# Key/query products in column strips, and the eight decay and gate columns computed from unsplit x, in a DeltaNet/HGRN2 layer on one core

## The chip, the cores and the metric

One NeuronCore of a Trainium2 chip runs the whole program in one launch. The metric is the device time of one execution in microseconds. The kernel before takes 2658.93 us, the median of three runs (2653.82 to 2660.26). Differences under about 0.3% (8 us) can't be told from no change with a few runs.

## The reference

One layer over 2048 tokens of width 1024. Its first part, where all of the change lies, is this (shapes: `GDN_HEADS` = 4, `HEAD_DIM` = 128, the DeltaNet works in chunks of 64 in the reference and of 128 in the kernel):

```python
hn = rms_norm(h, pre_mix_norm[i])
proj = jnp.einsum('btd,dc->btc', hn, w_in[i])     # 32 blocks of 128 columns, and 4 + 4 more
a_gdn = proj[..., OFF_GDN_A:OFF_GDN_B]            # 4 columns: decays
b_gdn = proj[..., OFF_GDN_B:OFF_HG_F]             # 4 columns: gates
...
beta = sigmoid(b_gdn)
g_dec = -exp(gdn_a_log[i]) * softplus(a_gdn + gdn_dt_bias[i])
gc = cumsum(g_dec)                                # inside each chunk
decay = exp(where(causal, gc[..., :, None] - gc[..., None, :], -inf))
lmat = einsum('bhncd,bhnsd->bhncs', k * beta, k) * decay   # only its strictly lower part is used
qk = einsum('bhncd,bhnsd->bhncs', q, k) * decay            # lower triangular
```

The DeltaNet heads, four HGRN2 heads (chunked too), an output projection, a squared-ReLU MLP of width 4096 and a gated embedding follow; the change does not touch what they compute.

## The kernel before

**Stages.** The tokens are worked in four quarters of 512 (`q`). First an embedding product runs while x is loaded and normed (lines L201, L439, L174/L175). Then comes the mixing stage: a list `works` holds, for each quarter, 1 + 8 x 4 = 33 products of the normed x with 128 columns of weights (`mm`, L1167). Output projection and MLP follow (L1050, L1200).

**A split product.** Weights and x are kept as a high and a low part (`split`: one ScalarE copy, L174, and one VectorE difference, L175), so a work is 8 x 3 = 24 matmuls of 128x512. The first work of each quarter, `ab`, has the eight columns of decays and gates in a block of 128 columns that are otherwise zero; it costs a whole work. In quarter 0 the weights are split and the split pair is stored (`cached`); later quarters reload 1 MB for each work.

**The clock.** Each work is three steps of eight matmuls. After every step `tick()` (after half a step `half()`) lets generators go on that stand in an `agenda` under that step: the recurrences of the eight heads (`gdn_mixer`, `hgrn_mixer`), loading of the next quarter's x (`load_x`), sums of MLP weights for later (`down_sums`), and `decays`. TensorE's and SyncE's order is the order of this code; ScalarE's, VectorE's and GpSimd's is set by a scheduler. `A_STEPS`, `B_STEPS`, `A_FIRST` and the like are the step offsets of the generators; a head has 24 steps.

**Full products and strips.** A 128x128 float32 matmul uses the whole array. `strip(g, ...)` is a float32 matmul with 32 stationary columns that lands on 32 rows of the result (`tile_position=(0, 32 g)`); the HGRN2 levels (`at_all`) and the DeltaNet solver (`psp`, `pst`, `psx`, `psd`) already use strips, four next to each other. In before, the k k and k q products of a head (`kk`, L688 and L689) are eight full 128x128 matmuls, and the HGRN2 diagonal (`at_h_d`, L884) is one full 128x256. A float32 matmul shows as two records in the trace.

**PSUM.** Eight banks: `pm` 2 (works), `pp` 3 (everything short: `kk`, `at_h_d`, transposes), `at_all` 1, `po` 2 (the output sums `pso` of a DeltaNet and of an HGRN2 head, in turn).

**Decays.** `decays` (L524 to L548) takes the sum of work `ab` as rows of 4 x 512: bias, softplus by Exp and Ln, tanh for the gates, a cumulative sum in four scans (L533), a store `gd` to DRAM from which each head reads its row as `gf` (L636), and four transposes `ps_gb` (L544) for the column form `gcol`.

Of the kernel before, what the change touches and what calls it, by code (L numbers as in the profile page):

```python
# [10 lines left out]
F32 = mybir.dt.float32  # L11
# [53 lines left out]

A_FIRST = (3, 7, 8, 8, 9, 10, 12, 14) + tuple(range(16, 24)) + (24, 26, 29, 32, 34, 36, 37)
# [30 lines left out]
def trunk(ctx, tc, x, xT, pT, vecs, w_in, w_ab, gdn_a_log, gdn_dt_bias, w_out, w_up, w_down,  # L97
# [12 lines left out]
    po = ctx.enter_context(tc.tile_pool(name="po", bufs=2, space=PSUM))  # L110
# [11 lines left out]
    V.memset(at_all, 0.0)  # L122
# [3 lines left out]
    dec = cp.tile([4, 2], F32, name="dec")  # L126
# [15 lines left out]
    nexpa = cp.tile([4, 1], F32, name="nexpa")  # L142

    def vectors():

        ps = bank("ps_rows", pp)
        PE.transpose(ps[:, :N_ROWS], rows, ident[:N_ROWS, :N_ROWS])
        V.tensor_copy(cols, ps[:, :N_ROWS])
        V.tensor_scalar(ple_w, cols[:, R_PLE : R_PLE + KD], 0.5, None, ALU.mult)
        V.tensor_tensor(lb, lg, lg, ALU.subtract)  # L150
        S.activation(lb, lb, AF.Exp)
        V.reciprocal(lb1, lb)
        V.tensor_tensor(lb, lb, lb1, ALU.mult)
        V.tensor_tensor(lb, lb, lb, ALU.subtract)
# [3 lines left out]
        S.activation(nexpa, dec[:, 0:1], AF.Exp)  # L158
        V.tensor_scalar(nexpa, nexpa, -1.0, None, ALU.mult)
# [227 lines left out]

    with ExitStack() as ectx:
        es = ectx.enter_context(tc.tile_pool(name="es", bufs=1))
        with tc.manual_schedule(engines={mybir.EngineType.SP, mybir.EngineType.Activation, mybir.EngineType.DVE}):  # L390
# [9 lines left out]
            nc.sync.dma_start(dec[:, 0:1], gdn_a_log.rearrange("o h -> h o"))  # L400
            nc.sync.dma_start(dec[:, 1:2], gdn_dt_bias.rearrange("o h -> h o"))
# [51 lines left out]
            while len(xts[0]) < KD:  # L453
                put_x()
            for f in stores:
                f()


    with mixers as mctx:
# [57 lines left out]
        gb = mt("gb", "gb", 1, (36, QT))  # L517
        V.memset(gb, 0.0)

        def decays(ps, q):  # L520

            sp = m2.tile([4, QT], F32, tag="tmp", name=f"sp_{q}")
            se = m2.tile([4, QT], F32, tag="th", name=f"se_{q}")
            S.activation(sp, ps[0:4, :], AF.Identity, bias=dec[:, 1:2])  # L524
            S.activation(gb[32:36, :], ps[32:36, :], AF.Tanh, scale=0.5)
            V.tensor_scalar(gb[32:36, :], gb[32:36, :], 0.5, 0.5, ALU.mult, ALU.add)
            V.scalar_tensor_tensor(se, sp, -1.0, sp, ALU.mult, ALU.max)
            S.activation(se, se, AF.Exp, scale=-1.0)
            S.activation(se, se, AF.Ln, bias=1.0)
            V.scalar_tensor_tensor(sp, sp, 0.0, se, ALU.max, ALU.add)  # L530
            V.tensor_scalar(sp, sp, nexpa, None, ALU.mult)
            for c in range(NC):
                V.tensor_tensor_scan(gb[0:4, blk(c)], one[0:4, :], sp[:, blk(c)], 0.0, ALU.mult, ALU.add)  # L533
            gd = dr.tile([4, QT], F32, name=f"gd{q}")
            decay[q] = [gd, None]
            yield
            nc.sync.dma_start(gd, gb[0:4, :])
            yield
            back = mt(f"gbb_{q}", "gbb", 1, (36, QT // 2))
            V.tensor_copy(back.rearrange("p (n b i) -> p n b i", b=NB, i=SB), odd_back(gb))  # L540
            yield
            ps = bank(f"ps_gb_{q}", ph)
            for c in range(NC):
                PE.transpose(ps[:, c * 36 : (c + 1) * 36], back[:, blk(c // 2)] if c % 2 else gb[:, blk(c)],  # L544
                             ident[:36, :36])
            gcol = sm.tile([P, NC, 36], F32, tag="gcol", name=f"gcol_{q}", bufs=2)
            V.tensor_copy(gcol.rearrange("p c n -> p (c n)"), ps[:, : NC * 36])
            V.tensor_scalar(gcol[:, :, 4:8], gcol[:, :, 0:4], -1.0, None, ALU.mult)  # L548
            decay[q][1] = gcol
# [81 lines left out]
        def gdn_mixer(q, h, live):  # L631
# [4 lines left out]
            nc.sync.dma_start(flat(gf), decay[q][0][h : h + 1, :].broadcast_to([P, QT]))  # L636
# [3 lines left out]
            beta = gcol[:, :, 32 + h : 33 + h].rearrange("p c o -> p (c o)")  # L640
# [43 lines left out]
            for c in range(0, NC, 2):  # L684
                ps = bank(f"kk_{n}_{c}", pp).rearrange("p (a b i) -> p a b i", a=2, b=2)
                for a in range(2):
                    sl = blk(c + a)
                    PE.matmul(ps[:, a, 0, :], kT[:, sl], kT[:, sl], start=True, stop=True)  # L688
                    PE.matmul(ps[:, a, 1, :], kT[:, sl], qT[:, sl], start=True, stop=True)  # L689
# [119 lines left out]
            pso = bank(f"pso_{n}", po)  # L809
# [40 lines left out]
        def hgrn_mixer(q, h, live):  # L850
# [26 lines left out]
            for lev, s in enumerate(LEVELS):  # L877
# [4 lines left out]
                if lev == 1:  # L882
                    ps0 = bank(f"at_{n}_d", ph)[:, : QT // 2]
                    PE.matmul(ps0, one, own, start=True, stop=True)  # L884
                    near = [slice(j * SB // 2, (j + 1) * SB // 2) for j in range(NB)]
                    ps1 = at_all.rearrange("p (c n) -> p c n", c=NC)
# [62 lines left out]
            pso = bank(f"pso_{n}", po)  # L949
# [64 lines left out]
        STEPS = SPT = 3  # L1014
        for q in range(NQ):
            works.append((f"ab{q}", "ab", w_ab, q, None, None, None, None))
# [61 lines left out]
        def load_x(q):  # L1078
# [11 lines left out]
            def ready(k):  # L1090
                t = ra.tile([P, 2, QT], F32R, tag="ring", name=f"xt{q}_{k}")
                split(t, V, raws.pop(k))
                xts[q].append(t)
# [18 lines left out]
            for k in range(2, KD):  # L1112
                ready(k)
                if k % 2:
                    yield

# [19 lines left out]
        per_q = SPT * (1 + 8 * 4)  # L1136
# [3 lines left out]
        for q in range(1, NQ):  # L1140
            at(per_q * (q - 1) + 30, x_scale(q), range(0, 22, 2))
            at(per_q * q, load_x(q), range(-9, 0))
            call(per_q * q, boundary)
        for q in range(2):
            at(0, norm_steps(accs[q], 1.0 / D, EPS, f"e{q}", partial(ple_r.__setitem__, q)),
               [4 * q + i for i in (0, 2, 4, 5, 6)])
        with tc.manual_schedule(engines={mybir.EngineType.SP}):
# [5 lines left out]
            for j, (name, key, src, q, h, then, g, b) in enumerate(works):  # L1153
# [9 lines left out]
                for s in range(SPT):  # L1163
# [4 lines left out]
                    if s == SPT - 1 and h is None:  # L1168
                        at(clock[0], decays(ps, q), (0, 2, 3, 5) if q else (0, 2, 4, 7))
                    tick()  # L1170
                    if s == SPT - 1 and h is not None:
                        then(ps, q, h, g, b)
# [10 lines left out]
    pp = ctx.enter_context(tc.tile_pool(name="pq", bufs=4, space=PSUM))  # L1183
    ctx.enter_context(tc.tile_pool(name="pad", bufs=1)).tile([P, 48], F32, name="pad")
# [790 lines left out]
```

## Time and profile before

| what | value |
|---|---|
| median of three runs | 2658.93 us |
| the profiled execution | 2650.4 us, span 2648.3 us |
| granted TensorE clock, mean | 0.998 |
| busy: TensorE, VectorE, ScalarE, GpSimd | 99%, 74%, 55%, 5% |
| records of matmuls | 14729 |
| mean DMA rate | 217 GB/s |

The page's busy time of TensorE is a union of modelled spans, so the end of each matmul overlaps the next one's start; what one matmul costs in a row of them is read from the distance of starts in the timeline. In a merged row of the timeline the first number is the start of its first record and "x16" the number of records.

### The profile page before, as it was taken

Reading aid. Unit: us, or ns where it says so; the run is one execution under the profiler, and the core shown is the slowest. Engines: PE = TensorE matmul, PEld = TensorE weight load, DVE = VectorE, ACT = ScalarE, POOL = GpSimd, SP = SyncE. Lnnn points to the kernel's source line nnn. Section 1 sums busy time; section 2 is a strip of 40 time slices with the busy share of each in tenths; the row PEclk is TensorE's granted clock in tenths of the full one; section 3 lists DMA queues with packets and bytes.
Section 4 is the critical chain, followed back from the end, with each engine's and each line's share of the span. In section 5 each row is a group of like instructions: output and inputs, shape, how many; then the busy total and the mean of one; then the engine's idle time right before and its main releaser. Section 6 shows DMA issues by size and latency. Waiting matters only on the chain.

```text
span 2648.3 us, 42218 instructions
## 1 busy us (share of the span) xinstructions
PE 2615.3 (99%) x14729; PEld 2159.7 (82%) x14729; DVE 1967.0 (74%) x4030; ACT 1467.4 (55%) x2991; POOL 138.1 (5%) x147
## 2 busy tenths in 40 slices
PE   8999999999999999999999999999999999999999
PEld 6788788888888888887888888888888888888887
DVE  7778777786777777678988778767877765477775
ACT  7676655565456555565666555555554555565431
POOL 0000000000000000110000000001000001101000
PEclk9999999999999999999999999999999999999999
DMA  7878777667667775773765476665644375677663
GB/s 275 273 254 274 249 252 261 226 224 255 218 212 243 226 230 175 212 229 123 235 212 197 171 238 222 215 208 194 207 159 169 138 247 186 199 251 253 202 225 127
DMA packets 267780, 573.75 MB, mean 217 GB/s; under 512 B 55578, under 2 KB 60152, under 8 KB 250416
## 3 DMA queue, kind: packets, MB, share of 16 engines
q1 hardware_dynamic: 265264, 566.86, 64.3%
q0 software_dynamic: 2304, 4.20, 0.9%
q8 instruction: 116, 1.90, 0.3%
q14 instruction: 96, 0.79, 0.1%
HBM read 410.57 MB, written 160.37 MB: 216 GB/s over the span
## 4 chain that ended last, share of the span: by engine, by line
PE 67%; DVE 3%; DMA 3%; issue 2%; ACT 1%; POOL 0%; SPq 0%; DVEq 0%; POOLq 0%; ACTq 0%
PE d L1200 23%; PE u L1200 23%; PE mm L1167 9%; PE mmg L1200 7%; PE mmo L1050 1%; PE mme L201 1%; DMA ud_g<-u_g 0%; DMA mixT<-mixd 0%; DMA yo<-in_xT_dram 0%; DMA xs<-in_x_dram 0%; POOL yo L1286 0%; DVE t L175 0%; DVE acc_o L244 0%; PE psc_g L823 0%; PE psa_g L813 0%
## 5 line engine op out<-in xcount | busy, mean ns | idle before, releaser
L1167 PE MATMUL mm<-xt,w 128*128 128x512 f32 x3072 | 785.4, 401 | 1.0 <-DVE w L175 0.9
L1167 PEld LDWEIGHTS mm<-xt,w 128*128 128x128 f32 x3072 | 552.6, 188 | 105.6 <-DVE w L175 1.7
L1200 PE MATMUL d<-db,da 128*128 128x512 f32 x2688 | 612.9, 389 | 0.0
L1200 PE MATMUL u<-t,wu 128*128 128x512 f32 x2604 | 591.2, 389 | 0.0
L1200 PEld LDWEIGHTS d<-db,da 128*128 128x128 f32 x2688 | 504.7, 188 | 104.6
L1200 PEld LDWEIGHTS u<-t,wu 128*128 128x128 f32 x2604 | 488.9, 188 | 101.3
L228 DVE TENSOR_TENSOR db<-db 128x512 fp32r<-128x512 f32 x224 | 159.8, 713 | 56.0 <-ACT db L227 55.2
L1598 DVE TENSOR_TENSOR u<-u,u 128x512 f32<-128x512 f32 x224 | 150.9, 685 | 53.0 <-PE u L1200 51.1
L1200 PE MATMUL mmg<-h2T,wg 128*128 128x512 f32 (+1 forms) x792 | 174.7, 383 | 0.0
L227 ACT ACTIVATE db<-db 128x512 fp32r<-128x512 f32 x224 | 141.0, 629 | 60.8 <-DMA db<-hid 57.2
L1200 PEld LDWEIGHTS mmg<-h2T,wg 128*128 128x128 f32 x792 | 145.6, 188 | 29.0
L1641 ACT ACTIVATE u<-u 128x512 f32<-128x512 f32 x128 | 80.7, 630 | 153.4 <-DVE u L1598 152.6
L175 DVE TENSOR_TENSOR da<-da 128x512 fp32r<-128x512 f32 x128 | 94.8, 740 | 89.6 <-ACT da L174 87.6
L174 ACT ACTIVATE da<-da 128x512 fp32r<-128x512 f32 x128 | 80.6, 629 | 127.2 <-DMA da<-sumd 105.4
L1200 PE MATMUL mmo<-mixT,w_out 128*128 128x512 f32 x600 | 138.5, 390 | 3.3 <-DVE w_out L175 1.7
L1200 PEld LDWEIGHTS mmo<-mixT,w_out 128*128 128x128 f32 x600 | 112.2, 188 | 28.6 <-DVE w_out L175 3.0
L174 ACT ACTIVATE wu<-a 128x512 fp32r<-128x512 f32 x124 | 75.0, 623 | 58.0 <-DMA a<-in_w_up_dram 55.7
L175 DVE TENSOR_TENSOR wu<-a,wu 128x512 fp32r<-128x512 f32 x124 | 86.3, 697 | 8.5 <-ACT wu L174 7.9
L175 DVE TENSOR_TENSOR da<-dr,da 128x512 fp32r<-128x512 f32 x96 | 68.3, 712 | 26.5 <-ACT da L174 25.4
L1642 ACT ACTIVATE u<-u 128x512 f32<-128x512 f32 x128 | 80.4, 628 | 3.0
L174 ACT ACTIVATE da<-dr 128x512 fp32r<-128x512 f32 x96 | 60.5, 630 | 33.6 <-DMA dr<-in_w_down_dram 26.8
L244 POOL TENSOR_TENSOR acc_y<-acc_y,sq_y 128x512 f32<-128x512 f32 x28 | 38.1, 1362 | 759.2 <-ACT sq_y L243 759.2
(394 smaller groups left out, 3722.7 us busy)
## 6 DMA issues: line engine op xcount, KB each, us to landing
w<-cache_in SPq DMA_DIRECT2D x96, 1024.0 KB
db<-hid SPq DMA_DIRECT2D x224, 256.0 KB
cache_in<-w SPq DMA_DIRECT2D x32, 1024.0 KB
hid<-u SPq DMA_DIRECT2D x128, 256.0 KB
da<-sumd SPq DMA_DIRECT2D x128, 256.0 KB
a<-in_w_up_dram SPq DMA_DIRECT2D x124, 256.0 KB
hid<-ht SPq DMA_DIRECT2D x96, 256.0 KB
dr<-in_w_down_dram SPq DMA_DIRECT2D x96, 256.0 KB
```

The lines of the kernel that those rows point to most:

```text
L174: S.activation(t[:, 0], raw, AF.Copy)
L175: eng.tensor_tensor(t[:, 1], raw, t[:, 0], ALU.subtract)
L201: PE.matmul(ps, a, b, start=i == 0, stop=i == n - 1)
L227: S.activation(t[:, 0], plain(t), AF.Copy)
L228: V.tensor_tensor(t[:, 1], plain(t), t[:, 0], ALU.subtract)
L244: eng.tensor_tensor(acc, acc, sq, ALU.add)
L1050: PE.matmul(ps, w[:, term // 2, k, :], xin[q][k][:, term % 2, :], start=i == 0, stop=i == 3 * KD - 1)
L1167: PE.matmul(ps, *terms[i], start=i == 0, stop=i == nt - 1)
L1200: PE.matmul(ps, a, b, start=start, stop=stop)
L1598: V.tensor_tensor(c[new], c[old], ps, ALU.add)
L1641: S.activation(c[k], c[k], AF.Relu)
L1642: S.activation(c[k], c[k], AF.Square)
```

## The change

1. The works `ab` go: 32 works in a quarter instead of 33 (`per_q` 99 to 96 steps), with their weight split, store and three reloads of 1 MB.
2. `few_columns` takes their place: for each 128 rows of x it runs four strips, one for each 128 tokens, with 32 stationary columns (`w_few`, of which 8 matter) and 128 moving columns of unsplit, float32 x. In quarter 0 these are 8 x 4 strips on the raw x at the end of the embedding; later 10 x 4 (the first two rows of x are taken as two halves each), one step before the quarter begins. The result has the tokens' four blocks on partitions 0, 32, 64 and 96.
3. `decays` works on that 128 x 128 form: one scan instead of four, the gates by Exp of the softplus instead of tanh, two copies on GpSimd and four 128x128 transposes. It is stepped at -0.5, 1 and 3 of the quarter (`FEW_STEPS`) instead of 2, 4, 5 and 7; `gf` is read as four 512-byte rows for each partition.
4. `kk`: eight full matmuls become 32 strips, each only as wide as the causal triangle needs (128, 96, 64, 32 columns), into two fixed banks `of_g` and `of_h`. These replace `po`: the DeltaNet output sum is always in `of_g`, the HGRN2 one in `of_h`. The HGRN2 diagonal becomes four strips of 64 columns into `of_h`.
5. `load_x` of the next quarter is stepped from -11 on instead of -9 (`X_STEPS`); its raw x is held until `few_columns` has read it.

```diff
+FEW_FIRST = (0, 2, 5)
+FEW_STEPS = (0.5, 2, 4)
+X_STEPS = (-11, -10, -9, -7, -6, -5, -3, -2, -1)
...
+    po = mixers.enter_context(tc.tile_pool(name="po", bufs=1, space=PSUM))
+    of_g, of_h = (po.tile([P, QT], F32, name=f"of_{n}") for n in "gh")
...
+    def few_columns(q, terms):
+
+        ps = bank(f"few_{q}", pp)[:, :P]
+        for i, (k, x) in enumerate(terms):
+            for c in range(NC):
+                PE.matmul(ps[c * SB : (c + 1) * SB, :], w_few[:, k * 8 : k * 8 + SB], x[:, blk(c)], start=i == 0,
+                          stop=i == len(terms) - 1, tile_position=(0, c * SB), skip_group_check=True)
+        return ps
...
+            few_first = few_columns(0, [(k, xraw[:, k]) for k in range(KD)])
...
+            sp, se, sums, beta = (mt(f"{n}_{q}", n, 1, (P, P)) for n in ("gsp", "gse", "gsum", "gbeta"))
+            S.activation(sp, ps, AF.Identity, scale=sign, bias=dec[:, 1:2])
             V.scalar_tensor_tensor(se, sp, -1.0, sp, ALU.mult, ALU.max)
             S.activation(se, se, AF.Exp, scale=-1.0)
             S.activation(se, se, AF.Ln, bias=1.0)
             V.scalar_tensor_tensor(sp, sp, 0.0, se, ALU.max, ALU.add)
+            S.activation(beta, sp, AF.Exp, scale=-1.0)
             V.tensor_scalar(sp, sp, nexpa, None, ALU.mult)
-            for c in range(NC):
-                V.tensor_tensor_scan(gb[0:4, blk(c)], one[0:4, :], sp[:, blk(c)], 0.0, ALU.mult, ALU.add)
+            V.tensor_tensor_scan(sums, one, sp, 0.0, ALU.mult, ALU.add)
...
             for c in range(0, NC, 2):
-                ps = bank(f"kk_{n}_{c}", pp).rearrange("p (a b i) -> p a b i", a=2, b=2)
-                for a in range(2):
-                    sl = blk(c + a)
-                    PE.matmul(ps[:, a, 0, :], kT[:, sl], kT[:, sl], start=True, stop=True)
-                    PE.matmul(ps[:, a, 1, :], kT[:, sl], qT[:, sl], start=True, stop=True)
+                ps = (of_h if c else of_g).rearrange("p (a b i) -> p a b i", a=2, b=2)
+                for b, src in enumerate((kT, qT)):
+                    for a in range(2):
+                        for g in range(NB)[:: -1 if a else 1]:
+                            first = slice(g * SB, P)
+                            if a:
+                                first = slice((NB - 1 - g) * SB, P) if b else slice(0, (g + 1) * SB)
+                            strip(g, ps[rows_of(g), a, b, first], kT[:, blk(c + a)][:, rows_of(g)], src[:, blk(c + a)][:, first])
...
-                    ps0 = bank(f"at_{n}_d", ph)[:, : QT // 2]
-                    PE.matmul(ps0, one, own, start=True, stop=True)
+                    ps0 = of_h[:, : QT // 2]
                     near = [slice(j * SB // 2, (j + 1) * SB // 2) for j in range(NB)]
+                    for j in range(NB):
+                        strip(j, ps0[rows_of(j)].rearrange("p (c n) -> p c n", c=NC)[:, :, near[j]], one[:, :SB],
+                              own.rearrange("p (c n) -> p c n", c=NC)[:, :, near[j]])
...
-            works.append((f"ab{q}", "ab", w_ab, q, None, None, None, None))
...
-        per_q = SPT * (1 + 8 * 4)
+        per_q = SPT * 8 * 4
...
-            at(per_q * q, load_x(q), range(-9, 0))
+            at(per_q * q, load_x(q), X_STEPS)
```

On TensorE, at the end of the embedding (`mme`) and the start of quarter 0, before:

```order
L201 MATMUL mme_7_546<-pT_1_363,w_plea_366 128x512 x3
L1167 MATMUL mm_ab_629<-xt_0_460,w_ab_614 128x512 x3
L1167 MATMUL mm_ab_629<-xt_1_477,w_ab_614 128x512 x3
L1167 MATMUL mm_ab_629<-xt_2_494,w_ab_614 128x512 x3
L1167 MATMUL mm_ab_629<-xt_3_511,w_ab_614 128x512 x3
```

and now, at the same place:

```order
L205 MATMUL mme_7_559<-pT_1_376,w_plea_379 128x512 x3
L397 MATMUL few_578<-xraw,w_few 32x128 x32
L1201 MATMUL mm_0_0_677<-xt_0_473,w_0_0_662 128x512 x3
L1201 MATMUL mm_0_0_677<-xt_1_490,w_0_0_662 128x512 x3
L1201 MATMUL mm_0_0_677<-xt_2_507,w_0_0_662 128x512 x3
```

The 24 matmuls on the split x (`xt`) have become 32 strips on the raw x, and the first head's own product follows at once.

On TensorE, before the k k and k q products of the second DeltaNet head of quarter 0, before (the rows ahead are the solver's and the HGRN2 strips of the head before):

```order
L629 MATMUL psx_g_0_1434<-part_582,xt_g_0_1206 32x32 x2
L629 MATMUL at_all<-qk_h_0_983,keys_h_0_3_1392 32x2x16 x8
L688 MATMUL kk_g_1_0_1473<-y_kg_1_1221 128x128
L689 MATMUL kk_g_1_0_1473<-y_qg_1_1297,y_kg_1_1221 128x128
L688 MATMUL kk_g_1_0_1473<-y_kg_1_1221 128x128
L689 MATMUL kk_g_1_0_1473<-y_qg_1_1297,y_kg_1_1221 128x128
```

and now (the first ten rows; 24 strips more follow):

```order
L654 MATMUL psx_g_0_1469<-part_628,xt_g_0_1245 32x32 x2
L654 MATMUL at_all<-qk_h_0_1022,keys_h_0_3_1427 32x2x16 x8
L654 MATMUL of_g<-y_kg_1_1260 32x128
L654 MATMUL of_g<-y_kg_1_1260 32x96
L654 MATMUL of_g<-y_kg_1_1260 32x64
L654 MATMUL of_g<-y_kg_1_1260 32x32
L654 MATMUL of_g<-y_kg_1_1260 32x128
L654 MATMUL of_g<-y_kg_1_1260 32x96
L654 MATMUL of_g<-y_kg_1_1260 32x64
L654 MATMUL of_g<-y_kg_1_1260 32x32
```

The products stand where they stood, right behind other strips, and each row of results has its own width.

On SyncE, where quarter 1's x is loaded, before (`raw_0_3` and `cache_in` are weights of quarter 0, `w_ab` and `w_1_0` reloads for quarter 1, `sys_g` and `ud_g` the solver's):

```order
L711 DMA sys_g_3_3097<-ud_g_3_3054 128x1x1024
L190 DMA cache_in_3109<-w_0_3_2912 128x2048
L255 DMA rsb_x_3121<-rd_x_1865 128x512
L1085 DMA raw_xt_0_3123<-in_xT_dram 128x512
L1085 DMA raw_xt_1_3125<-in_xT_dram 128x512
L620 DMA mixd_1_103<-og_g_1_2763 128x512
L1101 DMA raw_xt_2_3170<-in_xT_dram 128x2x512
L1101 DMA raw_xt_4_3172<-in_xT_dram 128x2x512
```

and now:

```order
L259 DMA rsb_x_3176<-rd_x_2001 128x512
L1115 DMA raw_xt_0_3178<-in_xT_dram 128x512
L1115 DMA raw_xt_1_3180<-in_xT_dram 128x512
L740 DMA sys_g_3_3209<-ud_g_3_3161 128x1x1024
L1131 DMA raw_xt_2_3211<-in_xT_dram 128x2x512
L1131 DMA raw_xt_4_3213<-in_xT_dram 128x2x512
L1115 DMA raw_xt_6_3219<-in_xT_dram 128x512
L194 DMA cache_in_3231<-w_0_3_2997 128x2048
```

The loads stand two steps earlier, now ahead of that weight store and around the solver's load instead of behind both; `raw_xt_4` takes the buffer of the quarter's last raw weights.

More of the change, by code (lines that the diff above doesn't have):

```diff
@@ L808, in gdn_mixer @@
             yield
-            pso = bank(f"pso_{n}", po)
+            pso = of_g
             for c in range(NC):
@@ L1113, in load_x @@
                 ready(k)
-                if k % 2:
+                if k % 2 and k + 1 < KD:
                     yield
+            halves = [(k, xts[q][k].bitcast(F32)[:, i, :]) for k in (0, 1) for i in range(2)]
+            at(clock[0], decays(few_columns(q, halves + [(k, raws[k]) for k in range(2, KD)]), q), FEW_STEPS)
+            yield
         def down_sums(g):
```

75 lines of the change are left out of this document (42 added, 33 removed).

## The prediction

> **What bounds the kernel now.** The page's head and its first part come first, then the busy time by stretch of the run, then who kept TensorE waiting.
>
> ```profile
> span 2648.3 us, 42218 instructions
> PE 2615.3 (99%) x14729; PEld 2159.7 (82%) x14729; DVE 1967.0 (74%) x4030; ACT 1467.4 (55%) x2991; POOL 138.1 (5%) x147
> 47.00:1023.00 976.00, 964.86 (x7278) 798.73 (x7278) 733.62 (x2096) 569.98 (x1480) 57.63 (x72) 1.00 0.73 242
> ```
>
> The last row is the mixing stage, where the whole change lies: 976 us, of which TensorE (first busy column) is free for 11 us. VectorE is busy 75% of it and ScalarE 58%, the granted clock is 1.00. The longest waits of TensorE by what ended them (total, times, longest):
>
> ```profile
> PE kk_g L689 <- ACT y_qg L576: 3.1, 4, 1.2
> PE psc_g L823 <- ACT w_g L820: 2.2, 2, 1.2
> PE kk_g L688 <- DVE xn_g L792: 2.0, 1, 2.0
> PE psp_g L629 <- DMA xn_g<-xd_g: 1.1, 1, 1.1
> ```
>
> So this stage is a full TensorE queue: work taken out of it should show nearly one for one, until the others become late. The sum is therefore one of TensorE time. It is made on the profiled execution (span 2648.3, time 2650.4 us), which lies 8.5 us under the median of 2658.93 and 3.4 us under the fastest of the three; I carry the difference over to the median.
>
> **Prices.** A split matmul of 512 columns:
>
> ```profile
> 2140.99 54.56 PE L1200 MATMUL d<-db,da 128*128 128x512 f32 x240
> ```
>
> is 0.227 us (54.56 less its tail, by 240). Full and strip float32 matmuls stand side by side here:
>
> ```profile
> 618.69 3.12 PE L1167 MATMUL mm<-xt,w 128*128 128x512 f32 x13
> 621.74 0.43 PE L629 MATMUL psp_g<-xn_g,um 128*32 128x64 f32 x16
> 621.99 0.31 PE L629 MATMUL at_all<-qk_h,keys_h 128*32 128x32 f32 x16
> 622.23 0.49 PE L688 MATMUL kk_g<-y_kg 128*128 128x128 f32 x2
> 622.55 0.39 PE L689 MATMUL kk_g<-y_qg,y_kg 128*128 128x128 f32 x2
> ...
> 623.89 0.39 PE L689 MATMUL kk_g<-y_qg,y_kg 128*128 128x128 f32 x2
> 624.04 2.33 PE L1167 MATMUL mm<-xt,w 128*128 128x512 f32 x9
> ```
>
> From 622.55 to 623.89 six full calls (two records each) start: 0.223 us a call, 1.74 ns a column. The 16 records of `psp_g` are eight strips of 64 columns, in 0.25 us: four such strips take 0.125 us, against 0.112 for one full call of that width. Strips in four column groups thus run at the same time, at 1.12 times the cost of one. Going into strips and back costs: 13 works' matmuls from 618.69 end at 621.64, the second `kk` call starts at 622.55, so the first would have stood at 622.33 in a row; of these 0.69 us the strips need 0.25 and about 0.13, and 0.31 is the change of mode. I use 0.33.
>
> **The works that go.** 4 x 24 x 0.227 = 21.8 us. The groups by line put them higher, since busy time holds the tails:
>
> ```profile
> L1167 PE MATMUL mm_ab<-xt,w_ab 128*128 128x512 f32 x96 | 24.6, 397 | 0.2 <-ACT sq_e L243 0.2
> L688 PE MATMUL kk_g<-y_kg 128*128 128x128 f32 x128 | 26.0, 285 | 2.0 <-DVE xn_g L792 2.0
> L689 PE MATMUL kk_g<-y_qg,y_kg 128*128 128x128 f32 x128 | 25.2, 278 | 3.1 <-ACT y_qg L576 3.1
> L884 PE MATMUL at_h_d<-att_h,one 128*128 128x256 f32 x32 | 9.5, 378 | 0.0
> ```
>
> I take 21.8. Their split, store and reloads (1 MB each) also go; neither was on the path, so that counts nothing.
>
> **The eight columns as strips.** 32 strips in quarter 0 and 3 x 40 after it: 152, or 38 sets of four, each 128 columns wide. No row shows strips of 128 columns. From below a set costs one full call, 0.223; from above four calls one after another, 0.89. I take 1.03 calls, near the 64-column row, as its 12% look like a fixed few ns: 38 x 0.23 = 8.7 us. Four entries and exits more, 1.3 us: together +10.0. The sets are one step ahead of the quarter, on x that was scaled four steps before, so they wait for nothing else.
>
> A rule speaks against so full an overlap. The Trainium skill, "TensorE: Matmul & The Clock Gate", Measured speedup vs the span model, has four row tiles 3.07 and three column tiles 2.38 times as fast as one by one, so some 1.26 to 1.3 calls for a set; by it this term would be about 11 us and not 8.7. The trace has 1.12 at 64 columns, which is better than the rule.
>
> **The HGRN2 diagonal.** Its full call of 256 columns is two of 0.223 = 0.446 us, and strips follow it at once, so no change of mode is added:
>
> ```profile
> 607.90 0.59 PE L884 MATMUL at_h_d<-att_h,one 128*128 128x256 f32 x2
> 608.42 0.46 PE L629 MATMUL at_all<-hb_h,qk_h 128*32 128x32 f32 x32
> ```
>
> Four strips of 64 columns cost the 0.125 of `psp_g`. 16 heads x 0.32 = -5.1 us.
>
> **The k k and k q products.** Now 8 x 0.223 = 1.79 us a head. As strips, two blocks give each column group 128 + 32 or 96 + 64 = 160 columns: 0.28 us if the groups run apart, 0.45 if each set of four waits for its widest. This row speaks for apart:
>
> ```profile
> 799.46 0.20 PE L629 MATMUL pst_g<-xt_g,part 128*32 128x32 f32 x3
> 799.48 0.22 PE L629 MATMUL at_all<-qk_h,keys_h 128*32 128x32 f32 x1
> 799.50 0.20 PE L629 MATMUL pst_g<-xt_g,part 128*32 128x32 f32 x2
> ```
>
> `at_all` is behind all `pst` in the program, and yet its first record starts before the last `pst`: a group that has less to do runs ahead. Four pairs: 1.12 to 1.79 us; I take 1.2, near the free end, so 16 x 0.59 = -9.4 us. In nearly all heads other strips stand directly ahead, so only one change of mode is added (+0.3).
>
> **Moved and hidden.** The new transposes are four of 128x128, as in the first row below, 0.36 us up to the next; the old four took 0.37. Even.
>
> ```profile
> 774.23 0.60 PE L597 MATMUL t_ih<-cst,iT_h 128*128 128x128 f32 x4
> 774.59 2.09 PE L1167 MATMUL mm<-xt,w 128*128 128x512 f32 x8
> 796.90 0.25 PE L544 MATMUL ps_gb<-cst,gb 36*128 36x36 f32 x1
> 797.27 0.50 PE L1167 MATMUL mm<-xt,w 128*128 128x512 f32 x1
> ```
>
> The decays' chain is what may now be late. Before, it ran from
>
> ```profile
> 783.86 0.66 ACT L524 ACTIVATE sp<-mm_ab,dec 4x512 f32<-4x512 f32 x1
> 785.16 1.28 ACT L528 ACT_TABLE_LOAD   x1
> 787.70 1.28 ACT L529 ACT_TABLE_LOAD   x1
> 791.33 1.35 DVE L533 TENSOR_TENSOR_SCAN gb<-one,sp 4x128 f32<-4x128 f32 x4
> ```
>
> to 792.68, 8.8 us, with 4 us in hand ahead of `ps_gb` at 796.90. Now operations have 128 columns instead of 512 and there is one scan (0.34), but one table load more (1.28) and the GpSimd copies: some 7 us. The transposes come 3.5 steps behind, at 976 / 396 = 2.46 us a step 8.6 us. Behind them on TensorE waits everything. It fits, narrowly; if the cover is gone, up to 3 us at each of three quarters.
>
> SyncE loads quarter 1's x into the buffer of the last raw weights, whose split is a step later; it stands there for about 2.5 us, with reloads behind it that are needed four steps later. I count nothing.
>
> The fixed banks could make TensorE wait for a reader. The DeltaNet sum was read here, and the products of the next but one head, which will share its bank, start here:
>
> ```profile
> 793.69 0.67 DVE L610 TENSOR_TENSOR og_g<-pso_g,zt_zg 128x512 f32<-128x512 f32 x1
> 810.88 0.39 PE L688 MATMUL kk_g<-y_kg 128*128 128x128 f32 x2
> ```
>
> 16.5 us lie between, three steps fewer now: still 9 us. Nothing.
>
> **Sum.** -21.8 + 10.0 - 5.1 - 9.4 + 0.3 = -26.0 us. The stage gets 2.7% shorter with almost the same work on VectorE and ScalarE, so its 11 us of waits will grow: +2.5, a guess at a fifth of them. Forecast: 23.5 us off, 2627 for a profiled execution and **2635** for the median.
>
> **Rivals.**
> - *Strips of 128 columns overlap only in part, or sets wait for their widest strip.* For it: no row has unequal strips or such wide ones. Against it: the run-ahead row. Strip work is 28 us at full overlap (8.5 + 16 x (1.12 + 0.11)); at 1.3 times that the gain is 8 us less, with the widest-strip rule for `kk` 9 us less: 2644. Chance 0.14. The skill's 2.38 and 3.07 above would give about this.
> - *Strips are held one after another by their issue or by the array: slower.* The place is the 32 strips of each head and the 38 sets. With 28 us at full overlap and 26 us of gain, the change breaks even where strips take 1.9 times as long as assumed; fully one by one (4 times) it costs 84 us more: 2717. Against it: 16 `psp_g` records in 0.25 us. Chance 0.06. The Trainium skill, same page, "Wait — 56ns, not 53.3ns?", has about 62 ns for each MATMUL with hardware decode off; for 1456 records that is 90 us. The trace disagrees: 16 ns a record.
> - *The decays' chain or the loads at the quarter's edge are late.* 3 us for the transposes and 1 to 2 for x at three edges: 12 us, 2647. Chance 0.06.
> - *The gain is taken back by VectorE at 75%* (or the change shifts less than it says): within 8 us of before. It would need waits of 18 us where there are 11 now. Chance 0.04.
>
> **How the numbers follow.** Forecast 0.70 and the rivals as above. About 0.3%, 8 us, is what can be told from no change: faster means under 2651. All of the forecast's 0.70, the first rival's 0.14 and two thirds of the third give 0.88; same 0.06; slower 0.06. The range goes from full overlap without new waits (-27.3, and the 5 us that the lowest run lies under the median, with a little for waits that vanish) at 2624 to the third rival with a margin, 2651; it leaves out the slower case, the last and some of the rest.
>
> **What would show it.** In the changed profile: no `mm_ab`; sets of four `few` strips 0.23 us apart; a head's 64 records of products within 1.1 to 1.3 us, where 1.8 would be the widest-strip case; `at_all` 0.13 us behind the diagonal; TensorE's free time in the stage still under 15 us; and `ps_gb` not waiting for GpSimd by more than 1 us. It is wrong if the stage is not some 20 us shorter, or if a wait on `of_g`, `of_h` or `ps_gb` shows over 3 us.

## The result, and the profile after

The change made the kernel slower: 2773.2 us in the median of four runs, against 2657.0 of the kernel before on the same chip, a ratio of 1.0444 (95% interval 1.0429 to 1.0459). The forecast was 2635. The head of the page of the changed kernel, profiled in a run of 2773.0 us:

```profile
span 2771.3 us, 44339 instructions
...
PE 2666.0 (96%) x15801; PEld 2165.9 (78%) x15801; DVE 1957.5 (71%) x4016; ACT 1467.6 (53%) x2996; POOL 142.4 (5%) x162
```

The busy time by stretch, first of the kernel before, then of the changed one. The first row of each goes from the first to the last matmul `mm` of the mixing stage, the second from there to the end. The first `ab` work before (41.07 to 46.64 us) and the first `few` strips now (43.55 to 45.44) lie ahead of these rows, so of the four `ab` works the first row holds three. The columns are length, then busy time of TensorE, its weight loads, VectorE, ScalarE and GpSimd, then granted clock, DMA share and GB/s.

```profile
47.50:1023.50 976.00, 965.02 (x7279) 798.84 (x7278) 733.62 (x2095) 569.88 (x1481) 57.13 (x68) 1.00 0.73 242
1023.50:2648.30 1624.80, 1614.47 (x7330) 1335.39 (x7328) 1197.80 (x1874) 865.09 (x1453) 77.52 (x64) 1.00 0.60 200
```

```profile
45.40:1120.10 1074.70, 990.53 (x8310) 806.18 (x8307) 724.70 (x2082) 571.62 (x1489) 63.06 (x86) 0.96 0.67 216
1120.10:2771.30 1651.20, 1643.67 (x7336) 1337.98 (x7334) 1199.54 (x1876) 865.91 (x1453) 77.03 (x64) 1.00 0.60 197
```

Two different things show. The mixing stage is 98.7 us longer: TensorE stands free for 84 us in it where it was 11, and the clock is 0.96. The rest, whose work the change does not touch, is 26.4 us longer, at clock 1.00 and with no more free time of TensorE than before (7.5 us, and 10.3 before).

**The strips themselves came out as forecast.** TensorE's timeline of the changed kernel, at the `few` strips of a quarter, at the 64 records of a head's products and at the HGRN2 diagonal (start, length, line, operation):

```profile
298.80 0.87 PE L1201 MATMUL mm<-xt,w 128*128 128x512 f32 x3
299.60 1.08 PE L397 MATMUL few<-xt,w_few 128*32 128x128 f32 x32
300.49 1.49 PE L397 MATMUL few<-raw_xt,w_few 128*32 128x128 f32 x48
301.92 1.19 PE L1201 MATMUL mm<-xt,w 128*128 128x512 f32 x4
...
615.72 0.31 PE L654 MATMUL at_all<-qk_h,keys_h 128*32 128x32 f32 x16
615.84 0.47 PE L654 MATMUL of_g<-y_kg 128*32 128x128 f32 x16
616.12 0.47 PE L654 MATMUL of_g<-y_qg,y_kg 128*32 128x128 f32 x16
616.40 0.47 PE L654 MATMUL of_h<-y_kg 128*32 128x128 f32 x16
616.68 0.47 PE L654 MATMUL of_h<-y_qg,y_kg 128*32 128x96 f32 x16
617.08 0.73 PE L1201 MATMUL mm<-xt,w 128*128 128x512 f32 x2
...
668.20 0.32 PE L654 MATMUL of_h<-att_h,one 128*32 128x64 f32 x8
668.34 0.48 PE L654 MATMUL at_all<-hb_h,qk_h 128*32 128x32 f32 x32
```

The 80 records are 40 strips of two records each, ten sets of four, in 2.32 us: 0.23 us a set. The products take 1.24 us a head (615.84 to 617.08), the diagonal 0.14 us.

**Where the mixing stage waits.** The waits of TensorE that grew most (total, times, longest), and ScalarE's wait for `gf`, before and after:

```profile
PE psc_g L852 <- ACT w_g L849: 44.1, 11, 6.4
PE psa_g L842 <- DVE S_g L854: 12.0, 7, 3.8
PE nrm_g L286 <- DVE hl_g L179: 5.4, 3, 4.4
```

```profile
ACT cd_g L645 <- DMA gf_g<-gd: 4.3, 3, 1.9
```

```profile
ACT cd_g L671 <- DMA gf_g<-gd: 104.4, 16, 10.2
```

VectorE stands for `gf` as well, 64.6 us at `tail_g`.

One of them in the timelines of SyncE's queue, ScalarE and TensorE:

```profile
630.18 0.47 SPq L662 DMA_DIRECT2D gf_g<-gd  x1
```

```profile
634.91 1.28 ACT L671 ACT_TABLE_LOAD   x1
645.75 0.21 ACT L671 ACTIVATE cd_g<-gf_g 128x4 f32<-128x4 f32 x1 [9.55 <-DMA gf_g<-gd]
...
648.26 0.34 ACT L849 ACTIVATE w_g<-psb_g,cc_g 128x128 f32<-128x128 f32 x1
```

```profile
641.76 1.18 PE L1201 MATMUL mm<-xt,w 128*128 128x512 f32 x4
648.66 0.79 PE L852 MATMUL psc_g<-w_g,kt_g 128*128 128x128 f32 x2 [5.71 <-ACT w_g L849]
```

`gf` of the next head is issued at 630.18 and is there at 645.7. ScalarE reaches `cd_g`, which reads it, at 636.2 and stands for 9.55 us. The next instruction of the current head's chain, `w_g`, is queued behind it on ScalarE: the product `psb_g` that it reads was done at 640.2, and it starts at 648.26. `psc_g` behind `w_g` stops TensorE for 5.7 us. So a load of the next head holds up the recurrence of this one.

**The clock adds to such waits.** Of a shorter wait, the row of TensorE and the stretches ahead of it and behind it:

```profile
985.17 0.49 PE L852 MATMUL psc_g<-w_g,kt_g 128*128 128x128 f32 x2 [1.97 <-ACT w_g L849]
```

```profile
980.00:983.00 3.00, 3.00 (x19) 2.45 (x18) 2.32 (x11) 0.41 (x2) 0.00 (x0) 1.00 0.65 203
986.20:989.50 3.30, 3.30 (x13) 3.00 (x12) 2.71 (x8) 1.38 (x5) 0.00 (x0) 0.50 0.89 341
```

After 1.97 us of waiting the granted clock is 0.50 for 3.4 us. Not each such wait has this effect: e1_row (below) has two of 2.0 and 2.1 us, and its clock stays at 1.00 behind both. The changed kernel has 17 such stretches of 3.4 to 10.2 us, each behind one or two waits; past the first 40 us, the kernel before has none up to its last matmul. They make 88.7 us, of which TensorE works 73.0; at half the clock some 36 us of that are lost, an estimate from these two figures. The Trainium skill, "TensorE: Matmul & The Clock Gate", HAM oscillation — how this bites in real kernels, warns of gaps above some 3.4 us; here 2 us were enough.

**The second half** has no new waits to show, only slower matmuls. One long row of it, before and after:

```profile
1849.04 292.11 PE L1200 MATMUL u<-t,wu 128*128 128x512 f32 x1288
```

```profile
1957.92 298.48 PE L1233 MATMUL u<-t,wu 128*128 128x512 f32 x1288
```

The same 1288 matmuls are 226.7 ns apart before and 231.6 ns after.

### The profile page after: what moved, and what is told of

It reads as the page before. It is cut to its first block, busy times and chain, and to the rows that moved or that the text cites. A ratio compares the mean times of both kernels' runs of the same rounds, so it can differ in the third digit from the quotient of the medians.

```text
span 2771.3 us, 44339 instructions
## 1 busy us (share of the span) xinstructions
PE 2666.0 (96%) x15801; PEld 2165.9 (78%) x15801; DVE 1957.5 (71%) x4016; ACT 1467.6 (53%) x2996; POOL 142.4 (5%) x162
## 4 chain that ended last, share of the span: by engine, by line
PE 53%; DVE 2%; issue 2%; DMA 2%; ACT 1%; POOL 0%; SPq 0%; DVEq 0%; POOLq 0%; ACTq 0%
PE u L1233 22%; PE d L1233 21%; PE mmg L1233 6%; PE mmo L1080 1%; PE mme L205 1%; DMA mixT<-mixd 0%; DMA sys_g<-ud_g 0%; DMA b<-h1d 0%; DMA yo<-in_xT_dram 0%; DVE acc_o L248 0%; POOL yo L1319 0%; DVE t L179 0%; DMA rd_g<-m_g 0%; DMA yod<-yo 0%; DVE w_out L179 0%
## 5 line engine op out<-in xcount | busy, mean ns | idle before, releaser
L1201 PE MATMUL mm<-xt,w 128*128 128x512 f32 x3072 | 819.1, 412 | 7.5 <-DVE w L179 2.5
L1201 PEld LDWEIGHTS mm<-xt,w 128*128 128x128 f32 x3072 | 567.9, 194 | 124.8 <-issue 4.4
L1233 PE MATMUL d<-db,da 128*128 128x512 f32 x2688 | 621.5, 392 | 0.1
L1233 PE MATMUL u<-t,wu 128*128 128x512 f32 x2604 | 604.0, 394 | 0.0
L179 DVE TENSOR_TENSOR wu<-a,wu 128x512 fp32r<-128x512 f32 x124 | 85.8, 694 | 10.6 <-ACT wu L178 10.4
```

Source lines behind the costliest of these rows:

```text
L179: eng.tensor_tensor(t[:, 1], raw, t[:, 0], ALU.subtract)
L1201: PE.matmul(ps, *terms[i], start=i == 0, stop=i == nt - 1)
L1233: PE.matmul(ps, a, b, start=start, stop=stop)
```

## The experiments

**1. What makes `gf` late.** The change stores the running sums as 128 rows of 128, so `gf` is read as four rows of 512 bytes per partition, 16,384 bytes apart in DRAM, where it was one row of 2 KB. Run e1_row puts the old form into the changed kernel:

```diff
-            gd = dr.tile([P, P], F32, name=f"gd{q}")
+            gd = dr.tile([4, QT], F32, name=f"gd{q}")
-            nc.sync.dma_start(gd, sums)
+            for c in range(NC):
+                nc.sync.dma_start(gd[:, blk(c)], sums[c * SB : c * SB + 4, :])
-            nc.sync.dma_start(gf, bass.AP(gd.tensor, gd.offset + h * P, [[0, P], [SB * P, NC], [1, P]]))
+            nc.sync.dma_start(flat(gf), decay[q][0][h : h + 1, :].broadcast_to([P, QT]))
```

> The changed kernel, with the running sums of the decays kept in DRAM as 4 rows of 512 again (four small stores, one per 128 tokens), so that `gf` is read as one row of 2 KB per partition and not as four of 512 bytes. Theory A (the read in small pieces makes `gf` late, and TensorE waits for what follows from it, with a lower clock after each wait): the 104 us that `cd_g` waits for it fall below 10, TensorE's waits in the mixing stage fall from about 130 us to about 40, the granted clock in that stage returns to 1.00, and the time falls by some 80 us, to about 2690. Rival (the decays' own chain of operations is what is late, whatever the form of the read): the time stays within 10 us of 2773.

Measured: 2686.4 us, 1.0124 [1.0098, 1.0149]; 87 us of the loss are gone and the clock is 0.999. But `cd_g` still waits nine times as long as before the change (e1_row, ScalarE's waits):

```profile
ACT cd_g L671 <- DMA gf_g<-gd: 37.5, 11, 5.5
```

So the form of the read is the largest cause and not the only one. Run e7_before_pieces gives the small pieces to the kernel before, 1 KB apart:

```diff
-            gd = dr.tile([4, QT], F32, name=f"gd{q}")
+            gd = dr.tile([4 * NC, 2 * P], F32, name=f"gd{q}")
+            nc.sync.dma_start(gf, bass.AP(gd.tensor, gd.offset + h * 2 * P * NC, [[0, P], [2 * P, NC], [1, P]]))
```

> The kernel before, with `gf` read as four rows of 512 bytes per partition from a DRAM tile with gaps, everything else as it was. Theory A: `gf` lands 6 to 9 us later, ScalarE waits for it at `cd_g` some 50 to 100 us in all, TensorE waits at `psc_g`, and the kernel takes 2700 to 2740. Rival (the pieces only hurt because the change had already made the heads' loads late): within 15 us of 2657.

Measured: 2658.0 us, 1.0011 [1.0000, 1.0023], and `cd_g` hardly waits:

```profile
ACT cd_g L647 <- DMA gf_g<-gd: 7.1, 3, 3.3
```

Theory A as I had put it is wrong: 512 packets of 512 bytes are not the trouble. The trace's DMA packets, the pieces in which a transfer moves, say what differs. Time from the first to the last of the 512 packets of one `gf`, over the 16 heads:

```
                     distance    median   shortest  longest   one packet
changed kernel       16,384 B    7.4 us     4.8      10.0       27 ns
e7_before_pieces      1,024 B    2.5 us     1.1       4.7       27 ns
e9_pitch             18,432 B    2.9 us     1.8       4.8       27 ns
e10_before_far       16,384 B    6.9 us     3.6      10.1       27 ns
```

The DMA engines are not full in this time. While the 512 packets of the `gf` shown above came, from 636.6 to 645.4 us, they were busy for 47% of it (the last column but one):

```profile
636.60:645.40 8.80, 6.34 (x36) 5.11 (x34) 3.84 (x15) 0.00 (x0) 0.00 (x0) 1.00 0.47 127
```

The last two runs of the table were made for this, from both sides. e9_pitch is the changed kernel with its DRAM rows 576 bytes apart:

```diff
-            gd = dr.tile([P, P], F32, name=f"gd{q}")
+            gd = dr.tile([P, P + 16], F32, name=f"gd{q}")
-            nc.sync.dma_start(gd, sums)
+            nc.sync.dma_start(gd[:, :P], sums)
-[[0, P], [SB * P, NC], [1, P]]
+[[0, P], [SB * (P + 16), NC], [1, P]]
```

> The changed kernel, with the rows of the DRAM tile of running sums 576 bytes apart instead of 512. `gf` is still read as four pieces of 512 bytes per partition, 512 packets in all, but the four pieces lie 18,432 bytes apart and not 16,384. In the changed kernel these packets take 27 ns each and yet 5 to 10 us from the first to the last; in the kernel before with pieces 1 KB apart the same 512 packets took 1.1 to 4.8 us. Theory A1 (it is the distance of 16 KB that makes them come slowly): the packets land within 3 us, `cd_g` waits some 40 us and not 104, the time falls by 70 to 85 us, to 2690 to 2705. Theory A2 (it is the number and size of the packets, in a kernel whose loads are late anyway): no change, 2765 to 2780.

Measured: 2694.8 us, 1.0154 [1.0141, 1.0167], as theory A1 has it; 64 bytes of pitch are worth 78 us. ScalarE's wait:

```profile
ACT cd_g L671 <- DMA gf_g<-gd: 40.0, 11, 6.6
```

e10_before_far is the kernel before with the changed kernel's layout of `gd` (128 rows of 128, the same read):

```diff
-            gd = dr.tile([4, QT], F32, name=f"gd{q}")
+            gd = dr.tile([P, P], F32, name=f"gd{q}")
+            nc.sync.dma_start(gf, bass.AP(gd.tensor, gd.offset + h * P, [[0, P], [SB * P, NC], [1, P]]))
```

> The kernel before, with the running sums stored and read in the changed kernel's layout: four pieces of 512 bytes per partition, 16,384 bytes apart. Theory A1: the packets take 5 to 10 us from first to last, ScalarE waits for `gf` at `cd_g` 50 to 100 us in all, and the time rises by 40 to 80 us, to 2695 to 2735. Theory A2: as with pieces 1 KB apart, within 10 us of the kernel before, 2655 to 2665.

Measured: 2714.4 us, 1.0226 [1.0213, 1.0239]: this layout alone costs an otherwise unchanged kernel 60 us. Its waits of ScalarE and of TensorE:

```profile
ACT cd_g L647 <- DMA gf_g<-gd: 62.0, 16, 8.2
```

```profile
PE psc_g L825 <- ACT w_g L822: 14.7, 5, 4.5
```

**2. What slows the matmuls of the second half.** Nothing in the instructions; but the tiles lie elsewhere. `w_few` and other small tiles add 384 bytes per partition to the pool of constants and a smaller `gcol` takes 768 off another pool. By the program's allocation, the pool `rb` of the MLP's x starts at byte 81,504 where it was 81,888, and the split weights' at 196,576 as before: modulo 256 (what is left of the byte address after division by 256), x lies at 96 and not at 224, and the weights at 224. Run e2_pad puts 128 unused bytes into the changed kernel, run e4_before_pad16 takes 128 bytes from an unused tile ahead of the MLP's pools in the kernel before, run e3_row_pad has the padding of e2_pad and the read of e1_row:

```diff
+    cp.tile([P, 32], F32, name="shift")          (e2_pad, e3_row_pad)
-    ctx.enter_context(tc.tile_pool(name="pad", bufs=1)).tile([P, 48], F32, name="pad")
+    ctx.enter_context(tc.tile_pool(name="pad", bufs=1)).tile([P, 16], F32, name="pad")     (e4_before_pad16)
```

> The changed kernel with an unused tile of 32 floats (128 bytes per partition) in the pool of constants, so that the pools behind it start at the same place modulo 256 bytes as in the kernel before (offset 224, where the change had made it 96). Theory B (matmuls whose operands lie at this other offset start later): the split matmuls of the MLP come back from about 230.5 ns to 226.7 ns, those of the mixing stage too; 11,000 of them by 4 ns are 44 us, so about 2729. Rival (the order of the PSUM pools, or something in the stream of instructions, slows them): spacing stays at 230 ns and the time at 2773.

> The kernel before with the unused tile ahead of the MLP's pools cut from 48 floats to 16, which moves these pools (x, products, results of the second half) down by 128 bytes and nothing else: offset 96 modulo 256 in place of 224. Theory B: the matmuls of the MLP go from 226.7 to about 230.5 ns, some 7000 x 4 ns = 28 us more: about 2685, with the mixing stage unchanged. Rival (PSUM order or the instructions): 2657, spacing 226.7 ns.

> The changed kernel with both: one row of 2 KB for `gf`, and the 128 bytes that restore the offsets. If theories A and B together are the whole loss, and the strips give what the forecast said, this comes out at about 2635, 0.992 of the kernel before. If the strips themselves cost time, it stays above 2657.

Measured: e2_pad 2744.9 us, 1.0340 [1.0316, 1.0364], 28 us less than the changed kernel, with the long row of `u` as it was before the change:

```profile
1944.51 292.11 PE L1234 MATMUL u<-t,wu 128*128 128x512 f32 x1288
```

It is not the 44 us expected. The matmuls of 512 columns in the mixing stage come sooner too (228.6 ns apart, 232.5 in the changed kernel), but the stage is only 2.2 us shorter and TensorE's free time in it is 93 us and not 84: what is gained there is waited away. e4_before_pad16 2679.4 us, 1.0093 [1.0067, 1.0118]: moving tiles by 128 bytes, and nothing else, costs the kernel before 23 us. Its long row of `u`:

```profile
1866.14 297.63 PE L1200 MATMUL u<-t,wu 128*128 128x512 f32 x1288
```

e3_row_pad 2660.8 us, 1.0021 [1.0006, 1.0036]: with both causes out the loss is gone, but so is the gain. Something takes some 25 us more than the forecast has (part 3).

Sorting the second half's matmuls of 512 columns by the places of their two operands modulo 256, taken from the programs' allocations, gives mean distances to the next start (where both neighbours are such matmuls):

```
                        moving operand / weights   matmuls   mean ns
kernel before               224 / 224               6076      226.7
changed kernel               96 / 96                 784      228.1
                            224 / 224               1606      227.7
                             96 / 224               3383      232.5
                            224 / 96                 535      232.8
```

The table suggests that the difference of the two counts and not the place. Whether the size of the difference matters it doesn't say. Three runs decide, on the fastest version of part 3, with 128 unused bytes at the weights' end of SBUF in place of the other end (both operands at 96), and with 64 and 96 unused bytes (differences of 64 and of 32 bytes):

```diff
-    cp.tile([P, 32], F32, name="shift")
+    ctx.enter_context(tc.tile_pool(name="shift", bufs=1, side="right")).tile([P, 32], F32, name="shift")     (s1_both_moved)
+    cp.tile([P, 16], F32, name="shift")     (s2_gap64)
+    cp.tile([P, 24], F32, name="shift")     (s3_gap32)
```

> The fastest version so far (2639 us), with its 128 unused bytes not in the pool of constants but at the other end of SBUF, ahead of the pools of split weights. So all operands of the split matmuls start at 96 modulo 256 bytes: those on the left where the change had put them, those on the right moved down to meet them. If the difference between the two operands is what counts: spacing 226.7 ns and 2635 to 2643 us. If the place itself counts (96 is slow, 224 is fast): 232 ns or more for all of them, 2665 to 2685.

> The fastest version, with an unused tile of 64 bytes in place of 128: the operands on the left start at 160, those on the right at 224 modulo 256, a difference of 64 bytes. If any difference costs the same: those matmuls whose operands differ take 232.5 ns, some 28 to 40 us in all, 2665 to 2680. If the cost goes with the difference: half of it, 229.6 ns and about 2655. If only 128 costs: 2639.

> The same with 96 bytes: 192 against 224, a difference of 32 bytes. Any difference: 232.5 ns, 2665 to 2680. In proportion: 228.1 ns, about 2647. Only 128: 2639.

Measured: s1_both_moved 2643.1 us, 0.9956 [0.9941, 0.9971], the matmuls of the second half 226.7 ns apart in the mean; s2_gap64 2673.9, 1.0068 [1.0047, 1.0089]; s3_gap32 2671.1, 1.0064 [1.0047, 1.0080]. The long row of s1_both_moved and that of s3_gap32:

```profile
1838.12 292.11 PE L1234 MATMUL u<-t,wu 128*128 128x512 f32 x1288
```

```profile
1853.96 299.08 PE L1234 MATMUL u<-t,wu 128*128 128x512 f32 x1288
```

So the difference counts, and 32, 64 and 128 bytes cost the same (about 233 ns). Multiples of 256 cost nothing: in the kernel before, pairs of 224 and 480 modulo 512 run at 226.7 ns.

**3. Where the gain went in e3_row_pad.** Its waits of ScalarE and of TensorE:

```profile
ACT cd_g L672 <- DMA gf_g<-gd: 39.3, 11, 5.7
```

```profile
PE psc_g L853 <- ACT w_g L850: 17.0, 12, 2.2
```

In the kernel before, the heads of a quarter began three steps after its start, since `ab` came first; now they begin at once. But the table of the sums over w_down, with its 1 MB loads, is counted from the quarter's start and kept its 5, so these loads now come three steps later against the heads. SyncE's queue shows them at the same head of the kernel before and of e3_row_pad:

```profile
432.07 0.93 SPq L1121 DMA_DIRECT2D wd<-in_w_down_dram  x2
...
448.90 0.43 SPq L636 DMA_DIRECT2D gf_g<-gd  x1
```

```profile
441.22 0.91 SPq L1155 DMA_DIRECT2D wd<-in_w_down_dram  x2
...
446.60 0.67 SPq L663 DMA_DIRECT2D gf_g<-gd  x1
```

The loads were issued 16.8 us ahead of `gf`, and now 5.4 us; in the DMA packets theirs are still under way when `gf` is issued, and it lands 9 us later and not 5. Run e5_sums_early sets the number back against the heads, e6_scale_early also that of x's scaling, e8_before_sums_late brings the offset into the kernel before:

```diff
-        starts = [per_q * q + 5 + n * i for ...]
+        starts = [per_q * q + 2 + n * i for ...]     (e5_sums_early, e6_scale_early; 8 in e8_before_sums_late)
-            at(per_q * (q - 1) + 30, x_scale(q), range(0, 22, 2))
+            at(per_q * (q - 1) + 27, x_scale(q), range(0, 22, 2))     (e6_scale_early)
```

> The repaired kernel (one row for `gf`, 128 bytes for the offsets), with one number changed: the sums over w_down's halves start at step 2 of a quarter and not at 5. The change took three steps (the `ab` work) from the head of each quarter, and this table kept its number, so its 1 MB loads of w_down came three steps later against the heads. Theory C (these loads now land in the DMA queues just ahead of `gf`, ScalarE stands at `cd_g`, and the `w_g` behind it lets TensorE wait at `psc_g`): the 39 us at `cd_g` fall to about 5, the 17 us of `psc_g` to about 3, the time from 2660 to about 2640. Rival D (ScalarE and TensorE wait because the strips and the missing work make TensorE faster, so that the chain of each chunk is bare): the waits at `psc_g` stay above 12 us and the time at 2655 or more.

> As the one before, and the scaling of the next quarter's x also three steps earlier (27 for 30), so that both stand against the heads as in the kernel before. Theory C: a few us less again (the loads of x for the square sums, `xs`, keep their old distance from `gf`): 2632 to 2640. Rival D: as the one before, 2655 or more.

> The kernel before, with the sums over w_down started three steps later (8 for 5), which is where the change left them against the heads. Theory C: `cd_g` waits 20 to 40 us for `gf`, `psc_g` waits 10 to 17 us, and the time rises by 10 to 25 us, to about 2675. Rival D: no more than 5 us, 2657 to 2662.

Measured: e5_sums_early 2647.0 us, 0.9972 [0.9962, 0.9983]; e6_scale_early 2648.3, 0.9976 [0.9965, 0.9988], no gain by the second number; e8_before_sums_late 2662.7, 1.0026 [1.0013, 1.0040], some 7 us slower by the ratio. That lies between theory C (10 to 25) and rival D (5 at most). The waits of e8_before_sums_late, then those of e5_sums_early:

```profile
ACT cd_g L645 <- DMA gf_g<-gd: 18.4, 6, 5.2
```

```profile
PE psc_g L823 <- ACT w_g L820: 4.9, 6, 1.5
```

```profile
ACT cd_g L672 <- DMA gf_g<-gd: 21.6, 10, 4.7
```

```profile
PE psc_g L853 <- ACT w_g L850: 6.6, 6, 1.9
```

The mechanism is there in both directions, at half the size that theory C gave or less: in e5_sums_early half of the wait at `cd_g` stays. So `gf` was issued two steps earlier as well:

```diff
-A_AHEAD = (-8, -6)
+A_AHEAD = (-10, -6)
```

> The kernel with one row for `gf`, restored offsets and sums three steps earlier (2647 us), with one more number changed: `gf` of a quarter's second to fourth head is issued 10 steps ahead and not 8, so 4.9 us earlier. Its buffer is free by then (its last reader ends some 10 us before the issue). Theory C: the 21.6 us at `cd_g` go, and with them the 6.6 us of `psc_g` and part of what follows: 2636 to 2642. Rival D (these waits come from other lateness): 2645 to 2650.

Measured: 2638.6 us, 0.9943 [0.9931, 0.9955], the fastest version, faster than both kernels. Its two rows that answer to those above, then its busy time by stretch:

```profile
ACT cd_g L672 <- DMA gf_g<-gd: 18.4, 10, 4.9
```

```profile
PE psc_g L853 <- ACT w_g L850: 2.6, 4, 0.8
```

```profile
45.40:1011.20 965.80, 946.27 (x8310) 778.78 (x8306) 719.42 (x2083) 567.23 (x1486) 62.73 (x86) 1.00 0.74 240
1011.20:2636.90 1625.70, 1615.06 (x7336) 1335.21 (x7334) 1194.83 (x1874) 865.86 (x1453) 76.85 (x64) 1.00 0.61 200
```

The second half is that of the kernel before, the stage is 10 us shorter. The time is in theory C's range, but its wait at `cd_g` did not go as expected (18.4 us are left of 21.6); it now hardly holds up `w_g`. `psc_g` accounts for 4 of the 8 us gained, and what gives the rest was not taken apart.

**4. What the strips are worth in the end.** e12_full_products is e5_sums_early with full calls for the products:

```diff
-                        for g in range(NB)[:: -1 if a else 1]:
-                            ...
-                            strip(g, ps[rows_of(g), a, b, first], kT[:, blk(c + a)][:, rows_of(g)], src[:, blk(c + a)][:, first])
+                        PE.matmul(ps[:, a, b, :], kT[:, blk(c + a)], src[:, blk(c + a)], start=True, stop=True)
```

> The same kernel (2647 us) with the products of k with k and with q as full calls of 128x128 again, in the fixed banks `of_g` and `of_h`. If the strips are worth what the trace of the changed kernel shows (1.24 us a head against 1.79) and this comes out in the end, it is 16 x 0.55 = 9 us slower: 2656. If the time that strips free on TensorE is only waited away behind VectorE and ScalarE, it stays at 2647 to 2650.

Measured: 2651.8 us, 0.9993 [0.9983, 1.0003]; 4.8 us slower than e5_sums_early by the medians and 5.6 by the ratios, between the two expectations. Some half of what the strips of the products free on TensorE arrives at the end; the two intervals meet at 0.9983, so the size is not known well.

The fixed causes add up from the medians: 2773.2, with the old read 2686.4 (-87), with the offsets 2660.8 (-26), with the sums earlier 2647.0 (-14), with `gf` issued earlier 2638.6 (-8). These medians are from different chips; by the ratios to the kernel before on the same chip the steps are 85, 27, 13 and 8 us. The last step is more than a repair: the kernel before has `gf` at 8 steps too, and what 10 would bring there was not tried.

## Why the prediction was wrong, step by step

- *The works that go, the eight columns, the diagonal, the products.* Right piece by piece: no `mm_ab` is left, 0.23 us a set (taken 0.23), 0.14 us a diagonal (0.125), 1.24 us a head (1.2). The strips run apart, also with unequal widths: both strip rivals are out. The Trainium skill's lower overlap ("TensorE: Matmul & The Clock Gate", Measured speedup vs the span model) would have made 0.28 to 0.29 us of a set; the trace has 0.23.
- *The decays' chain fits, narrowly.* Right: no wait of TensorE at `ps_gb` shows.
- *The fixed banks: nothing.* Right, though the sign that was named for the contrary, a wait over 3 us, did show once. It is for `y_qg` of ScalarE, and not for a reader of the bank:

```profile
PE of_g L654 <- ACT y_qg L601: 3.8, 1, 3.8
```

- *Moved and hidden.* This step failed. It costed the transposes, the chain, x's loads and the banks, and left out three things that the diff contains. The `gf` read has a new form, and stood nowhere in the sum; it costs 60 us in a kernel that is otherwise the one before (e10_before_far) and 87 in this one (e1_row). Tables counted from the quarter's start, of which one was not moved with the heads, brought loads ahead of `gf` (14 us, e5_sums_early; 7 in the kernel before, e8_before_sums_late). And new tiles in an old pool move every tile behind them, which costs 23 to 28 us (e4_before_pad16, e2_pad).
- *The waits grow by 2.5 us.* Wrong by 70: TensorE's free time in the stage went from 11 to 84 us. "Almost the same work on VectorE and ScalarE" was true and did not matter: ScalarE is free for nearly half of the stage and still sets its end, since it takes its instructions in order and one of them stands for a DMA.
- *The rival of loads that are late at the quarter's edge* had the right kind of cause, but only at three edges and for 12 us. The read is late in every head, at all 16.
- *What would show it* named the stage's free time below 15 us; 84 is the line that told at once. A clock below 1.00 was not on the list.

With the three causes repaired and `gf` earlier, the profiled span is 11.4 us below that of the kernel before, where 23.5 were forecast; the medians on one chip differ by 15.9. Of the span's 11.4 us, TensorE's busy time gives 21.8 (2615.3 to 2593.5), where the sum had 26.0, and its free time takes 10.4 back, where the sum had 2.5. Of these 10.4, the first 100 us have 5.6 (17.6 us free, 12.0 before). The rest is spread over short waits on many lines; neither it nor the 4 us of busy time was taken apart.

## What to carry to other kernels

A change on paper of one engine's work must be read for everything it moves: each DMA whose access pattern changes, each table that counts from a point which has moved, and the place of each tile behind a pool that grows or shrinks. What stands for a DMA on an in-order engine is worth what is queued behind it, so ask of each load of the next head what of this head waits behind its first reader. When a whole stage gets slower by a constant few per cent with no waits and the clock at 1.00, compare the operands' places, not the instructions.

## What the runs showed of the hardware

- A split matmul of 512 columns whose moving operand and weights start at different places modulo 256 bytes comes 232.5 to 233 ns after the one before, not 226.7; differences of 32, 64 and 128 bytes cost the same, and the place itself nothing. The Trainium skill, "SBUF — State Buffer", Who interferes with whom, gives TensorE two independent read ports, one for the moving operand and one for the weights, and has it wait for nobody; the measured 6 ns hang on how the two operands lie to each other, which speaks against full independence. Where the two meet, and which of them waits, is not shown.
- Reads of four 512-byte pieces by 128 partitions take 6.9 to 7.4 us when the pieces are 16,384 bytes apart in DRAM, and 2.5 to 2.9 us at 1,024 or 18,432 bytes, with 27 ns for the packet itself in all cases. Other distances were not tried. In which part of the memory's path they queue is not shown.
- 2 us without matmuls in the middle of a busy stage can halve the granted clock for the next 3.4 us (985 us in the changed kernel), and need not (two waits of e1_row). The longest stretches at half the clock are 10.2 us.
